# Fetching modulation matrix tiles one product ahead, spreading their products over four blocks, and storing the HGRN masks once

## The chip, the cores and the metric

The kernel runs on one core of one Trainium2 chip. The metric is the device time of one execution in microseconds (us); for several runs the median is given. All other times below are read from one profiled execution.

## The reference

One decoder layer over 2048 positions of width 1024. What matters here is the modulation vector, the in-projection that it feeds, and the three mixers behind it:

```python
c_act = jax.nn.silu(c)
mod = c_act @ ada_w[l] + ada_b[l]
sh1, sc1, g1, sh2, sc2, g2 = [m[:, None, :] for m in jnp.split(mod, N_MOD, axis=-1)]
h = rmsnorm(x, norm_mix_w[l]) * (1.0 + sc1) + sh1
proj = h @ w_in[l]
o_a = hgrn2_mixer(hq, hf, hi, hg, lower_bounds[l], hg_onorm_w[l])
o_b = dsa_mixer(sq, sk, sv, iq, ik, iw)
o_c = conv_module(cu, cv_w[l], cv_b[l], cv_ln_w[l], cv_ln_b[l])
x = x + g1 * (jnp.concatenate([o_a, o_b, o_c], axis=-1) @ w_out[l])
h = rmsnorm(x, norm_mlp_w[l]) * (1.0 + sc2) + sh2
x = x + g2 * (jnp.square(jax.nn.relu(h @ mlp_w1[l])) @ mlp_w2[l])
```

`ada_w` is a 1024 x 6144 matrix in f32. Sections 0 and 1 (`sh1`, `sc1`) are needed before the first in-projection; sections 2 to 5 (`g1`, `sh2`, `sc2`, `g2`) only behind the in-projection. The HGRN mixer works in chunks of 128 positions and masks its products level by level with 0/1 masks (`lmask`), one for each of five levels.

## The kernel before

**Blocks.** The 2048 positions are four blocks of 512. `in_block(b, ...)` runs the in-projection of a block as 26 units: each unit is a matmul against one slice of `w_in` (L357, or L1165 for the wide ones), followed by an evacuation (`ev_hf`, `ev_hq`, `ev_ca` ...). After the fourth block come the out-projection and the MLP, which use sections 2 to 5 of the modulation.

**Work beside the units.** At each bare `yield` of `in_block`, `step()` gives a credit in ns to seven queues of generators (`rates`): `fast` (HGRN, `hgrn_gen`), `conv` (`conv_gen`), `ada` (`ada_gen`), `idx`, `tk`, `at` (indexer, top-k, attention) and `ts`. A generator runs as long as its queue has credit and says at each yield how much that piece costs. So the order of the program is: unit, evacuation, some HGRN, some conv, some modulation, and so on. From this order a planner lays out one instruction order for each engine; it may put an instruction ahead of earlier ones if its inputs and its buffer are there, and it plans with its own durations. On the chip each engine runs its instructions strictly in that order, SyncE (SP) its DMA issues too.

**Modulation, sections 2 to 5.** `ada_gen` walks 4 sections x 4 column slices of 256. Each slice is a sum of 8 products, done by `ada_part`: for k in 0..7 it takes a 128 x 256 tile of `ada_w` (128 KB, tag `adw`, AB = 2 buffers) by a DMA on SP (L186) and multiplies it on VectorE (DVE) by one column of `cact`, at L188 for k = 0 and at L190 (multiply and add into `adacc`, one buffer) for the other seven. Then TensorE (PE) sums over partitions: at L707 into one row in sections 2 and 5, to which L710 adds a slice of `ada_b` (tile `adrow`, which has the tag `adw` too) before a DMA stores it in `g_d`; at L198 into columns in sections 3 and 4, read by L199. Both take a bank of the tag `mm`, which the units of the in-projection use as well. A product asks for 1.2 x 256 = 307.2 ns of credit; the rate is 800 a step. `ada_gen` is queued in block 1 (behind unit 2, event "idx"), and at the event "prep" (block 3, ahead of unit 14) the queue is drained.

**Conv.** `conv_gen` multiplies 31 taps into two accumulators: half of the taps on DVE (L530, 128 x 512, `cacc`), half by ScalarE (ACT) and GpSimd (POOL) (L527, L528).

**HGRN.** `hgrn_gen` works on one head of a block. Per level it multiplies q and k by gates (L604, L605; the factor is read by repeat), PE makes the level's product (L639, L647), and for levels 0 to 4 DVE copies the masked part (L620, L641, `copy_predicated`). `lmask` holds 5 x 256 bytes per partition: the mask of 64 columns, four times over. It is made at the start by `late_consts` with a 128 x 256 work tile `mwork` (tag `r`, one buffer; L445 to L450). The head's result is a tile `r` of the same tag (L694), stored to `mx_d` by a DMA.

## Time and profile before

| what | value |
|---|---|
| time, median of 3 runs | 3066.41 us (3060.03 to 3070.0) |
| time of the profiled execution | 3064.96 us |
| its span, first to last instruction | 3063.2 us |
| mean granted TensorE clock | 0.966 of 2.4 GHz |
| PE busy | 2831.0 us, 92% of the span |
| DVE busy | 1982.8 us, 65% |
| POOL busy | 1792.8 us, 59% |
| ACT busy | 1541.4 us, 50% |
| DMA, share of 16 engines' time in the main queue | 57.5% |

The profiled execution lies 1.45 us below the median, inside the spread of the runs; 1.8 us of it lie outside the span. PE, DVE, ACT, POOL and SP are the five engines; a name such as "DVE k L605" is the instruction of line 605 on VectorE that writes tile `k`. "A <- B" in a list of waits means that A's engine sat idle until B was done. "PEclk" is the share of full clock granted to TensorE.

### The profile page before, as it was taken

To read this page: it belongs to the slowest core of one execution; us is meant where nothing else is said; L and a number is where in the kernel's file an instruction comes from. 1 tells how busy PE (TensorE), PEld (TensorE's weight loads), DVE (VectorE), ACT (ScalarE), POOL (GpSimd) and SP (SyncE) were. 2 spreads that over 40 slices of the span, in tenths; PEclk is the share of its full clock that TensorE was granted. 3 is DMA by queue.
4 is the path that set the end of the run, shared out by engine and by line. 5 is a ranking of instruction groups with operands and counts; after the bars stand their busy time and mean duration, and the time that the engine had idled before them with its cause. 6 is when DMAs were issued, how large, how long until landed. Compare 5 with 4: busy or idle time off the path is not lost.

```text
span 3063.2 us, 50800 instructions
## 1 busy us (share of the span) xinstructions
PE 2831.0 (92%) x18352; PEld 2554.6 (83%) x18352; DVE 1982.8 (65%) x3673; ACT 1541.4 (50%) x2883; POOL 1792.8 (59%) x1530
## 2 busy tenths in 40 slices
PE   6989989898999989999999999998899998989997
PEld 4768868777887889888988899898788887889997
DVE  7796487867536343756667747476979531387787
ACT  3436355445423244555556656555654444456654
POOL 6566152225304265666788666577776756767775
PEclk9989989898999999999999999999999999999999
DMA  7857757565655343444556445344899953465533
GB/s 258 283 183 244 229 182 228 190 202 172 227 185 166 119 156 100 130 126 131 167 154 212 138 135 154 121 157 159 259 302 291 320 184 118 139 196 183 176 125 114
DMA packets 479416, 560.10 MB, mean 183 GB/s; under 512 B 32615, under 2 KB 371884, under 8 KB 479148
## 3 DMA queue, kind: packets, MB, share of 16 engines
q1 hardware_dynamic: 478992, 556.65, 57.5%
q8 instruction: 145, 2.38, 0.3%
q14 instruction: 123, 1.01, 0.1%
q10 hardware_dynamic: 156, 0.07, 0.0%
HBM read 458.30 MB, written 98.31 MB: 182 GB/s over the span
## 4 chain that ended last, share of the span: by engine, by line
PE 47%; DVE 8%; DMA 4%; issue 4%; POOL 3%; ACT 2%; SPq 1%; DVEq 0%; POOLq 0%; ACTq 0%
PE ax L1165 18%; PE mm L357 14%; PE ix L752 1%; PE po L939 1%; PE at L905 1%; PE at L927 1%; DMA tsr<-in_mlp_w_dram 1%; PE mm L1165 1%; PE at L1165 1%; POOL wlo L264 1%; PE ax L1530 1%; PE at L1541 1%; PE ax L1541 1%; SPq L106 1%; PE at L1530 1%
## 5 line engine op out<-in xcount | busy, mean ns | idle before, releaser
L264 POOL TENSOR_TENSOR wlo<-wraw,whi 128x512 fp32r<-128x512 f32 x514 | 719.3, 1420 | 406.8 <-ACT whi L256 269.6
L256 ACT CAST whi<-wraw 128x1024 fp32r<-128x1024 f32 x257 | 269.5, 1049 | 329.0 <-PE ax L1165 137.8
L759 DVE SCALAR_TENSOR_TENSOR s<-r,iw_s,s 128x512 f32<-128x512 f32 (+3 forms) x266 | 261.9, 984 | 209.7 <-ACT r L754 208.5
L1165 PE MATMUL ax<-whi,hh 128*128 128x256 f32 x1600 | 282.5, 290 | 30.4 <-DVE acc L1309 20.7
L357 PE MATMUL mm<-ah,wk 128*128 128x512 f32 x1104 | 299.3, 407 | 9.0 <-ACT k L577 3.5
L1165 PE MATMUL ax<-whi,hl 128*128 128x256 f32 x1600 | 280.5, 288 | 2.4 <-POOL hl L264 2.4
L1165 PE MATMUL ax<-wlo,hh 128*128 128x256 f32 x1600 | 274.0, 287 | 0.0
L937 POOL TENSOR_TENSOR pT<-L,pT 128x512 fp32r<-128x512 f32 (+3 forms) x160 | 197.5, 1237 | 130.7 <-ACT pT L936 111.2
L1165 PEld LDWEIGHTS ax<-whi,hh 128*128 128x128 f32 x1600 | 235.8, 193 | 39.8 <-DVE acc L1309 19.6
L357 PE MATMUL mm<-ah,whi 128*128 128x512 f32 x936 | 255.7, 399 | 10.3 <-DVE slo L470 3.0
L357 PE MATMUL mm<-al,whi 128*128 128x512 f32 x936 | 258.6, 398 | 0.0
L357 PEld LDWEIGHTS mm<-ah,wk 128*128 128x128 f32 x1104 | 208.2, 194 | 55.1 <-ACT k L577 4.5
L357 PE MATMUL mm<-ah,wlo 128*128 128x512 f32 x936 | 253.0, 394 | 0.0
L1165 PEld LDWEIGHTS ax<-whi,hl 128*128 128x128 f32 x1600 | 233.5, 193 | 5.6 <-POOL hl L264 3.2
L1165 PEld LDWEIGHTS ax<-wlo,hh 128*128 128x128 f32 x1600 | 231.2, 193 | 2.6
L754 ACT ACTIVATE r<-ix 128x512 f32<-128x512 f32 (+3 forms) x256 | 141.2, 552 | 181.2 <-PE ix L752 168.3
L528 POOL TENSOR_TENSOR cside<-cside,ctap 128x512 f32<-128x512 f32 x112 | 161.3, 1440 | 115.0 <-ACT ctap L527 92.0
L357 PEld LDWEIGHTS mm<-ah,whi 128*128 128x128 f32 x936 | 174.2, 190 | 47.1 <-DVE slo L470 3.9
L357 PEld LDWEIGHTS mm<-al,whi 128*128 128x128 f32 x936 | 176.2, 191 | 35.3
L357 PEld LDWEIGHTS mm<-ah,wlo 128*128 128x128 f32 x936 | 175.1, 189 | 35.9
L1309 DVE TENSOR_TENSOR acc<-acc,ax 128x512 f32<-128x512 f32 x160 | 109.1, 682 | 96.4 <-PE ax L1165 96.1
L857 DVE TENSOR_SCALAR_CACHE_REDUCE cum<-s,ssm 128x384 bf16<-128x384 f32 (+13 forms) x112 | 165.2, 1475 | 5.0 <-POOL s L763 3.1
(552 smaller groups left out, 6842.6 us busy)
## 6 DMA issues: line engine op xcount, KB each, us to landing
wraw<-in_mlp_w_dram SPq DMA_DIRECT2D x192, 512.0 KB
wk<-wk_d SPq DMA_DIRECT2D x174, 512.0 KB
kc<-sk_d SPq DMA_DIRECT2D x112, 256.0 KB
vc<-v_d SPq DMA_DIRECT2D x112, 256.0 KB
tsr<-in_mlp_w_dram SPq DMA_DIRECT2D x96, 256.0 KB
ts_d<-tsr SPq DMA_DIRECT2D x48, 512.0 KB
wr<-in_mlp_w_dram SPq DMA_DIRECT2D x96, 256.0 KB
wr<-ts_d SPq DMA_DIRECT2D x72, 256.0 KB
```

The lines of the kernel that those rows point to most:

```text
L256: A.copy(hi, src)
L264: e.tensor_tensor(lo[:, i:j], src[:, i:j], hi[:, i:j].bitcast(F32), OP.subtract)
L357: T.matmul(ps, ww[:, k, :], aa[k], start=(n == 0 and k0 == 0), stop=(n == len(order) - 1 and k1 == NK))
L528: G.tensor_tensor(side, side, tap, OP.add)
L754: A.activation(r[:, :w], ps[:, :w], AF.Relu, scale=32.0 ** -0.5)
L759: V.scalar_tensor_tensor(s[:, c0:c0 + w], r[:, :w], iw, s[:, c0:c0 + w], op0=OP.mult, op1=OP.add)
L857: V.tensor_scalar(dump, s, t, -AIM - i * STEP, op0=OP.is_ge, op1=OP.add, accum_out=d)
L937: G.tensor_tensor(pT[:, :nt, 1], lv, pT[:, :nt, 0].bitcast(F32), OP.subtract)
L1165: T.matmul(ps[:, t * 256:(t + 1) * 256], aa[f][:, tok * P:(tok + 1) * P], ww[:, f, :], start=(first and n == 0 and (last or t == 0)), stop ...
L1309: V.tensor_tensor(dst, dst, src, OP.add)
L1530: T.matmul(dst, ww[:, k, :], av[k][p], start=(first and n == 0), stop=(n == 11), skip_group_check=True)
L1541: T.matmul(dst[:, t], av[k][p][:, t * P:(t + 1) * P], ww[:, k, :], start=(first and n == 0), stop=(n in (5, 11)), skip_group_check=True)
```

## The change

1. The tiles of `ada_w` come from a generator of their own, `ada_tiles`, which allocates a tile and issues its DMA one product before that tile is handed out. `adw` gets 3 buffers instead of 2.
2. `adrow` takes the tag `r` (the HGRN result's, one buffer) instead of `adw`.
3. `ada_gen` is queued in block 0 instead of block 1, and its rate is 400 a step instead of 800.
4. `lmask` holds the 64 columns of each mask once and is read by repeat (a step of 0) at L620 and L641; `mwork` shrinks to 128 x 64 with it.

```diff
-WQ, AQ, AB = 0, 0, 2
+WQ, AB = 0, 3
...
-    def ada_part(pool, wtag, wbufs, acc, sec, c0, w):
+    def ada_tiles():
+
+        todo = [(sec, c0, k) for sec in (2, 4, 3, 5) for c0 in range(0, D, AW) for k in range(NK)]
+        ahead = []
+        for sec, c0, k in todo:
+            t = hp.tile([P, AW], F32, tag="adw", bufs=AB, name=nm("adw"))
+            dma(t, ada2[k * P:(k + 1) * P, sec * D + c0:sec * D + c0 + AW])
+            ahead.append(t)
+            if len(ahead) > 1:
+                yield ahead.pop(0)
+        yield ahead.pop(0)
+
+    def ada_part(acc, tiles):
         for k in range(NK):
-            t = pool.tile([P, w], F32, tag=wtag, bufs=wbufs, name=nm("adw"))
-            (nc.gpsimd if AQ else nc.sync).dma_start(t, ada2[k * P:(k + 1) * P, sec * D + c0:sec * D + c0 + w])
+            t = next(tiles)
             if k == 0:
                 V.tensor_scalar(acc, t, cact[:, 0:1], None, op0=OP.mult)
             else:
                 V.scalar_tensor_tensor(acc, t, cact[:, k:k + 1], acc, op0=OP.mult, op1=OP.add)
-            yield 1.2 * w
+            yield 1.2 * AW
...
-    lmask = cst.tile([P, 5, 256], U8, name="lmask")
+    lmask = cst.tile([P, 5, 64], U8, name="lmask")
...
-        mwork = hp.tile([P, 256], F32, tag="r", bufs=1, name="mwork")
+        mwork = hp.tile([P, 64], F32, tag="r", bufs=1, name="mwork")
...
-            G.affine_select(mwork, mwork, pattern=[[0, 4], [-2 * h, ng], [0, h]],
+            G.affine_select(mwork, mwork, pattern=[[-2 * h, ng], [0, h]],
...
-                              lmask[:, 0, :128].rearrange("p (c g) -> p c g", c=2), pv[:, :, P:])
+                              lmask[:, 0:1, :].to_broadcast([P, 2, 64]), pv[:, :, P:])
...
-                                  lmask[:, l, :].rearrange("p (c g e) -> p c g e", c=4, e=hs), psv)
+                                  lmask[:, l:l + 1, :].rearrange("p o (g e) -> p o g e", e=hs)
+                                  .to_broadcast([P, 4, gc, hs]), psv)
...
     def ada_gen():
+        tiles = ada_tiles()
...
-                yield from ada_part(hp, "adw", AB, acc, sec, c0, AW)
+                yield from ada_part(acc, tiles)
...
-                    row = hp.tile([1, AW], F32, tag="adw", bufs=AB, name=nm("adrow"))
+                    row = hp.tile([1, AW], F32, tag="r", bufs=1, name=nm("adrow"))
...
-    rates = {"fast": FAST, "conv": CR, "ada": 800.0, "ts": 1.0, "idx": R1[0], "tk": R1[1], "at": R1[2]}
+    rates = {"fast": FAST, "conv": CR, "ada": 400.0, "ts": 1.0, "idx": R1[0], "tk": R1[1], "at": R1[2]}
...
                 if b == 0:
                     add_topk(k1, (2, 3))
+                    queues["ada"].append(ada_gen())
                 if b == 1:
                     add_topk(k1, range(4, J1))
-                    queues["ada"].append(ada_gen())
```

## Rows read from the trace of the kernel before

**Rows 1.** The page's first part: busy time of each engine and its share.

```profile
PE 2831.0 (92%) x18352; PEld 2554.6 (83%) x18352; DVE 1982.8 (65%) x3673; ACT 1541.4 (50%) x2883; POOL 1792.8 (59%) x1530
```

**Rows 2.** Blocks 0 to 3: stretch, length, PE, PEld, DVE, ACT, POOL busy, PEclk, DMA share, GB/s.

```profile
65.00:307.00 242.00, 217.68 (x1213) 186.50 (x1214) 181.96 (x375) 118.32 (x218) 145.66 (x124) 0.94 0.72 233
307.00:576.00 269.00, 246.16 (x1447) 209.70 (x1447) 191.93 (x471) 131.50 (x297) 87.15 (x99) 0.94 0.65 205
576.00:843.00 267.00, 243.36 (x1445) 207.32 (x1445) 181.79 (x428) 121.78 (x265) 93.72 (x93) 0.95 0.63 203
843.00:1085.00 242.00, 232.13 (x1465) 206.06 (x1464) 117.99 (x219) 69.23 (x155) 71.11 (x63) 0.98 0.48 157
```

**Rows 3.** Waits of DVE from 0 to 1150 us: total, times, longest.

```profile
DVE adacc L190 <- DMA adw<-in_ada_w_dram: 57.9, 38, 6.4
```

**Rows 4.** Waits of PE from 307 to 843 us (blocks 1 and 2): total, times, longest.

```profile
PE ax L647 <- DVE k L605: 11.5, 3, 4.6
```

**Rows 5.** Instructions on tile adw: durations ns min/median/max, first and last start.

```profile
L190 DVE SCALAR_TENSOR_TENSOR adacc<-adw,cact,adacc x112: 469/485/1615, 50.9 to 776.3; 128x256 f32<-128x256 f32 x112
```

**Rows 6.** DVE in order of time, block 1: start, length, [idle before <- ended by].

```profile
385.67 0.48 DVE L190 SCALAR_TENSOR_TENSOR adacc<-adw,cact,adacc 128x256 f32<-128x256 f32 x1 [1.88 <-DMA adw<-in_ada_w_dram]
...
388.14 0.52 DVE L190 SCALAR_TENSOR_TENSOR adacc<-adw,cact,adacc 128x256 f32<-128x256 f32 x1 [1.26 <-DMA adw<-in_ada_w_dram]
```

**Rows 7.** PE in order of time, block 1.

```profile
397.59 3.78 PE L357 MATMUL mm<-ah,wk 128*128 128x512 f32 x8 [3.04 <-ACT k L577]
...
426.06 0.92 PE L647 MATMUL ax<-q,k 128*64 128x64 f32 x8 [4.36 <-DVE k L605]
```

**Rows 8.** DVE in order of time, block 2: first and last of four waits.

```profile
736.97 0.48 DVE L190 SCALAR_TENSOR_TENSOR adacc<-adw,cact,adacc 128x256 f32<-128x256 f32 x1 [2.95 <-DMA adw<-in_ada_w_dram]
...
742.00 0.48 DVE L190 SCALAR_TENSOR_TENSOR adacc<-adw,cact,adacc 128x256 f32<-128x256 f32 x1 [0.88 <-DMA adw<-in_ada_w_dram]
```

**Rows 9.** PE in order of time, block 2.

```profile
752.11 0.80 PE L905 MATMUL at<-kc,qs 128*128 128x256 f32 x2 [5.04 <-DVE mx L907]
```

**Rows 10.** Two stretches of 10 us, columns as in Rows 2.

```profile
390.00:400.00 10.00, 6.70 (x30) 4.96 (x29) 10.00 (x14) 6.27 (x11) 5.32 (x5) 0.78 0.55 183
...
750.00:760.00 10.00, 7.89 (x47) 7.90 (x47) 6.52 (x19) 2.61 (x6) 2.85 (x4) 0.66 0.42 139
```

**Rows 11.** The conv stretch of each block, columns as in Rows 2.

```profile
120.00:190.00 70.00, 58.93 (x261) 47.21 (x262) 69.39 (x120) 27.53 (x49) 44.67 (x33) 0.88 0.61 199
390.00:434.00 44.00, 30.99 (x148) 23.05 (x146) 44.00 (x73) 22.09 (x40) 23.34 (x21) 0.83 0.52 164
660.00:720.00 60.00, 52.47 (x263) 41.33 (x262) 57.43 (x102) 29.30 (x61) 30.98 (x26) 0.89 0.56 183
910.00:955.00 45.00, 39.06 (x194) 30.94 (x193) 44.23 (x58) 15.83 (x26) 21.43 (x15) 0.96 0.41 131
```

**Rows 12.** The same stretches of blocks 1 and 2, tile adacc alone: PE, PEld, DVE busy.

```profile
390.00:434.00 44.00, 1.40 (x4) 0.17 (x4) 7.92 (x9) 0.83 0.52 164
660.00:720.00 60.00, 1.63 (x6) 0.70 (x6) 12.07 (x16) 0.89 0.56 183
```

**Rows 13.** Groups by line, until 307 us and in block 1: busy, mean ns | idle before.

```profile
L190 DVE SCALAR_TENSOR_TENSOR adacc<-adw,cact,adacc 128x256 f32<-128x256 f32 x7 | 5.3, 760 | 0.1
...
L190 DVE SCALAR_TENSOR_TENSOR adacc<-adw,cact,adacc 128x256 f32<-128x256 f32 x56 | 33.2, 593 | 33.4 <-DMA adw<-in_ada_w_dram 33.1
```

**Rows 14.** Tile lmask's largest group, columns as in Rows 5.

```profile
L641 DVE COPY_PREDICATED at<-lmask,ax x64: 418/436/754, 113.8 to 1107.7; 128x256 f32<-128x256 uint8 x64
```

**Rows 15.** DVE in order of time: the start, then two 256-wide operations of block 1.

```profile
29.26 0.29 DVE L450 CAST lmask<-mwork 128x256 uint8<-128x256 f32 x1 [0.54 <-POOL mwork L448]
...
392.46 0.41 DVE L605 TENSOR_TENSOR k<-k,fb 128x256 f32<-128x256 f32 x1
...
407.24 0.41 DVE L655 TENSOR_TENSOR fb<-f 128x256 f32<-128x256 f32 x1
```

**Rows 16.** Waits of SP's DMA queue from 307 to 790 us: total, times, longest.

```profile
SPq L186 <- DVE adacc L190: 46.8, 43, 5.2
```

More of the change, by code (lines that the diff above doesn't have):

```diff
@@ L445, in late_consts @@
             V.memset(mwork, 1.0)
-            G.affine_select(mwork, mwork, pattern=[[0, 4], [-2 * h, ng], [0, h]],
+            G.affine_select(mwork, mwork, pattern=[[-2 * h, ng], [0, h]],
                             compare_op=OP.is_ge, fill=0.0, base=0, channel_multiplier=1)
-            G.affine_select(mwork, mwork, pattern=[[0, 4], [2 * h, ng], [0, h]],
+            G.affine_select(mwork, mwork, pattern=[[2 * h, ng], [0, h]],
                             compare_op=OP.is_gt, fill=0.0, base=h, channel_multiplier=-1)
```

## The prediction

> **What bounds the kernel now.** The page's first part comes first: PE is busy 92% of the span and no other engine is over 65% [rows 1]. So a microsecond on another engine counts only where PE then stands still, or where the granted clock falls behind such a stall. The change touches the start and the four in-projection blocks alone, so next I read the blocks [rows 2]. Blocks 1 and 2, which hold all but the first eight of the 128 products, leave PE idle 22.8 and 23.6 us. Block 0, without those, is no better: 24.3 us. Block 3, without modulation and with little attention beside it, has 9.9 us. DVE's busy time goes with that: 182, 192, 182 and 118 us.
>
> Who waits for whom is the third view. Over the in-projection DVE stands still 57.9 us, in 38 waits, for `adw` tiles [rows 3]; PE itself never waits for them, but for DVE's later work, above all L605 [rows 4]. A DVE wait costs something only if it stands ahead of a PE stall with no slack between. Two places in the order of time show that. In block 1, waits of 1.88 and 1.26 us [rows 6] open a run in which DVE has no more idle time until 434 us, and in that run PE stalls, 3.04 and 4.36 us at the two largest [rows 7]. In block 2, four waits that add up to 4.97 us (first and last of the four in [rows 8], the other two are of 0.54 and 0.60 us) come before a PE stall of 5.04 us that DVE's L907 ends [rows 9]. Behind these stalls the granted clock is 0.78 and 0.66 of 2.4 GHz in the 10 us around them [rows 10]: part of that time is at the level of 1.2 GHz.
>
> **The change part by part.**
>
> *Prefetch.* Before, SP issues tile k+2 only when product k has freed its buffer: its L186 waited 46.8 us for L190 [rows 16], and the product that follows meets a tile still in flight. With a third buffer and one product ahead, three tiles are under way instead of two. At 1.3 products a step of 8 to 9 us (400 / 307.2; 242 us / 29 steps in block 0), a product comes every 6.4 to 7 us, longer than any wait of the 38 (6.4 us at most). I take the waits as gone. What it is worth is the part that stands before a stall: 1.88 + 1.26 in block 1 and 4.97 in block 2, 8.1 us. The clock behind them lost (1 - 0.78) x 10 = 2.2 and (1 - 0.66) x 10 = 3.4 us; the stalls of block 1 don't vanish, so I take half of 5.6. Together -8.1 - 2.8 = **-10.9 us**; bounds 0 (another releaser is as late) and -13.7.
>
> *Spread.* In program order the products go from 0, 68, 60, 0 in the four blocks to 34, 38, 38, 18 (26, 29, 29 and 15 steps). What counts is the conv stretch of each block, where DVE is busy 96 to 100% and PE idles 11.1, 13.0, 7.5 and 5.9 us [rows 11]. There the modulation now takes 0, 7.92, 12.07 and 0 us of DVE [rows 12]. After, at a product every 6.4 us in block 0 and 7.1 us in the others, the stretches hold 11, 6, 8 and 6 of them instead of 0, 9, 16 and 0. A product costs 0.76 us by the mean of the few in block 0 and 0.59 in block 1 [rows 13]; in the stretches themselves 7.92 / 9 = 0.88 and 12.07 / 16 = 0.75. So DVE's load there moves by +11 x 0.76 = +8.4, -3 x 0.88 = -2.6, -8 x 0.75 = -6.0 and +6 x 0.75 = +4.5, in sum +4.3 us. How much reaches PE: in the stretches PE idles 37.5 us of 219 (the four of [rows 11]), far less than DVE is full, so a DVE microsecond is not a PE microsecond. Between 0 (a product fits where DVE idles soon after the stretch) and 1 with the clock on top, I take half and a third of that again for the clock: **+2.9 us**; bounds 0 and +12.
>
> *What a product costs in block 0.* The row: L190 takes 0.469 us at best, 0.485 in the median and 1.615 at most [rows 5], and POOL, which reads SBUF too, is busy 60% of block 0 against 32% of block 1 [rows 2]; the means stand in the same order. The Trainium skill (SBUF — State Buffer, "SBUF: two separate sides") says that a VectorE operation with two SBUF inputs and a GpSimd operation that reads SBUF exclude one another for the whole instruction. That speaks against moving products into the block where GpSimd is busiest. By the rule, with half of a 1.3 us POOL operation to wait out in 60% of cases, an estimate from that page's rule is 0.48 + 0.39 = 0.87 us a product, and the stretch of block 0 would take 9.6 us instead of 8.4; the trace agrees as far as its means go.
>
> *Row tile on tag `r`.* Eight `adrow` tiles now share one buffer with the 16 HGRN results. A row's load waits on SP until the last result is stored, with the weights queued behind it, and the next L694 on DVE waits until the row is stored. No row of before shows that wait. It is nothing if the planner has a row and a result apart; at the worst it is a wait like those of the `adw` tiles, 57.9 / 38 = 1.5 us, for each of eight rows, half of them before a stall: +6 us. I take 0, since results are a head apart (some 65 us) and a row lives a few us.
>
> *Masks.* Ten POOL and ten DVE operations at the start get a quarter as wide. DVE waited 0.54 us for one of them and spent 0.29 on the copy [rows 15], in the chain that leads to the first projections; there are five. I take **-1.5 us**, bounds 0 and -3. Reading by repeat: the 64 L641 take 0.436 us in the median [rows 14]; none of before repeats a mask. The nearest is L605, which reads a factor by repeat and takes 0.41 us, as L655 does with plain inputs of the same width [rows 15]. So 0; if 0.03 us came on each of 96 (L641's 64 and L620's 32), +3 us of DVE, of which half at most counts.
>
> *DMA.* Block 0 gets 26 more tiles of 128 KB, 3.4 MB beside the 56 MB that it moves (233 GB/s x 242 us): the share goes from 0.72 to some 0.76. The cover is the weights' own lead: no weight's DMA stands among PE's waits there. 0; without that cover, 3.4 MB at 233 GB/s are 15 us of transfer.
>
> Sum against the profiled execution: 3064.96 - 10.9 + 2.9 - 1.5 = 3055.5. That execution lies 1.45 us below the median of the runs, which is less than their spread, so I leave it: **3055 us**, 0.37% under the median. Its own range, with all bounds: -16.7 to +22.5, say 3048 to 3080, the upper part only if the price of block 0 goes to its bound.
>
> **The rivals.**
>
> *Block 0 decides (slower).* Its conv stretch has DVE busy 69.4 of 70 us with PE idle 11.1 already [rows 11]; nothing is left there to hide 11 products, and two slice sums fall into it, each holding one of the units' two `mm` banks until DVE adds the row. If each added microsecond reaches PE, with half again for the clock (0.88 there already), block 0 costs 8.4 x 1.5 = 12.6 and block 3, in the same way, 4.5 x 1.5 = 6.8; blocks 1 and 2 give back the waits without the clock, 8.1. Sum +11: **3076 us**. It decides from the point where PE's idle time between 120 and 190 us grows beyond some 20 us. For it: the full DVE. Against: DVE has half of the 10 us after 190 us free, and block 1 with 7.9 us of products in 44 us has only 2 us more PE idle than block 0's stretch.
>
> *The waits change places.* Where DVE doesn't wait for a tile it runs into the next wait of its strict order, for PE or ACT, and the stalls stay: block 0 has as much PE idle without any tile to wait for. Gain 0 there, the spread about 0: **3065 us**.
>
> *The prefetch doesn't do what it says.* The planner may already lay products in bursts as soon as buffers are free, so that three buffers only shorten the waits (57.9 x 2/3 = 39 us left), and one product ahead is no time ahead. A third of the 8.1 us is won: **3062 us**.
>
> *More than counted.* The whole run of stalls in block 1 (13.0 us idle, clock 0.83 over 44 us = 7.5 us) and the one of block 2 (5.0 + 3.4) go: -25, **3040 us**.
>
> **How the numbers follow.** Chances: forecast 0.47, block 0 decides 0.22, waits change places 0.15, prefetch idle 0.08, more than counted 0.08. About 0.3% (9 us) is what a measurement of this kernel can tell from no change. The forecast lies at that edge: I give its chance as 0.28 faster, 0.17 same, 0.02 slower. With 0.08 of the last rival and 0.04 of the two small ones, faster is 0.40; same is 0.17 + 0.19 and 0.02 of the block 0 case, 0.38; slower the rest, 0.22. The range takes in both neighbours, from near the large gain to beyond the slower case: 3042 to 3080.
>
> **What would show it.** Right: the `adw` waits of DVE fall below 15 us; the stall at 752 us is gone and the clock of its 10 us near 1; PE idle in blocks 1 and 2 falls by 4 to 5 us each and in block 0 rises by no more than 5. Wrong: PE idle in block 0 up by 9 us or more; new waits of L694 for the row's store; L641 slower than 0.44 us; or waits of the same size in blocks 1 and 2 with another releaser. A different order that the planner lays out for work the change doesn't touch would make the whole sum wrong.

## The result, and the profile after

The changed kernel takes **3099.27 us** (median of 4 runs, 3093.52 to 3101.09) against 3066.36 us beside it: a ratio of **1.0105 [1.0088, 1.0121]**. It is slower by 1%, 44 us above the forecast and outside the range. Lines move with the change: L190 is now L201, L605 L616, L641 L652, L694 L706, L707 L720, L710 L723, and the DMA on SP L106.

The page's first part of the profile after, beside [rows 1]: with as many instructions PE is busy 9.3 us longer and DVE 15.7; the span is 3097.0, 33.8 us longer.

```profile
PE 2840.3 (92%) x18352; PEld 2556.1 (83%) x18352; DVE 1998.5 (65%) x3673; ACT 1536.8 (50%) x2885; POOL 1778.9 (57%) x1530
```

Where do 33.8 us lie? Busy times by stretch, columns as in Rows 2: the in-projection (up to the fourth store of `x_d`), the MLP of the first block (up to its fourth store of the output), and the rest, first before and then after.

```profile
0.00:1105.90 1105.90, 993.78 (x5872) 856.87 (x5872) 727.74 (x1594) 472.80 (x977) 457.03 (x442) 0.95 0.63 203
1105.90:1655.00 549.10, 528.02 (x3394) 478.24 (x3395) 345.09 (x691) 305.62 (x552) 373.28 (x321) 0.98 0.47 144
1655.00:3063.20 1408.20, 1309.24 (x9087) 1219.52 (x9085) 909.93 (x1390) 763.00 (x1355) 962.50 (x769) 0.97 0.58 183
```

```profile
0.00:1135.30 1135.30, 1004.25 (x5874) 867.37 (x5875) 731.22 (x1594) 473.93 (x981) 446.40 (x442) 0.94 0.61 197
1135.30:1690.50 555.20, 530.90 (x3409) 479.06 (x3409) 350.46 (x697) 308.45 (x554) 370.16 (x321) 0.98 0.47 143
1690.50:3097.00 1406.50, 1305.12 (x9073) 1209.67 (x9071) 916.77 (x1383) 754.46 (x1352) 962.35 (x769) 0.97 0.59 182
```

The in-projection is 29.4 us longer, the first MLP block, whose code is untouched, is 6.1 us longer, and the rest is 1.7 us shorter. Now the four blocks of after, to be read against [rows 2] (a block runs here from ACT's first write of tile `kst` to the next one, the last to the fourth store of `x_d`; the same bounds in before give 242.3, 269.7, 265.6 and 262.8 us, behind a start of 65.5, now 60.5):

```profile
60.50:343.10 282.60, 235.68 (x1261) 198.24 (x1260) 208.23 (x426) 124.05 (x232) 147.48 (x131) 0.89 0.67 219
343.10:599.50 256.40, 239.15 (x1409) 205.97 (x1407) 175.57 (x425) 134.29 (x295) 85.28 (x95) 0.95 0.61 196
599.50:866.60 267.10, 240.09 (x1428) 208.73 (x1428) 174.08 (x402) 115.36 (x259) 91.20 (x92) 0.94 0.59 195
866.60:1135.30 268.70, 253.59 (x1634) 224.94 (x1634) 129.76 (x251) 75.78 (x165) 86.14 (x79) 0.97 0.48 157
```

**Block 0 is 40.3 us longer.** PE idles 282.6 - 235.7 = 46.9 us in it instead of 24.2, and the granted clock is 0.89 instead of 0.94 over a longer time: (1 - 0.89) x 282.6 = 31 us lost instead of 15. A part is work that changed sides of the mark: block 0 holds 1261 matmuls, and 1217 before by the same bounds. Block 1 gives 13.3 us back, block 2 has 1.5 more, block 3 has 5.9 more.

The waits of DVE and of PE from 0 to 1150 us (total, times, longest), beside [rows 3, 4]:

```profile
DVE adacc L201 <- DMA adw<-in_ada_w_dram: 40.8, 24, 5.5
```

```profile
PE ax L650 <- DVE k L616: 28.0, 8, 8.9
```

The waits for `adw` fell from 57.9 to 40.8 us only. PE's waits for DVE's gates, the second fence, grew to 28.0 us (behind L605 before they were 21.0 over the same stretch).

### The profile page after: what moved, and what is told of

It is laid out like the page before. It is cut to its first block, busy times and chain, and to the rows that moved or that the text cites. A ratio compares the mean times of both kernels' runs of the same rounds, so it can differ in the third digit from the quotient of the medians.

```text
span 3097.0 us, 50847 instructions
## 1 busy us (share of the span) xinstructions
PE 2840.3 (92%) x18352; PEld 2556.1 (83%) x18352; DVE 1998.5 (65%) x3673; ACT 1536.8 (50%) x2885; POOL 1778.9 (57%) x1530
## 4 chain that ended last, share of the span: by engine, by line
PE 56%; DVE 19%; DMA 8%; issue 6%; POOL 6%; ACT 3%; SPq 1%; DVEq 0%; POOLq 0%; ACTq 0%
PE mm L368 20%; PE ax L1178 17%; PE mm L1178 3%; DVE cacc L541 3%; POOL wlo L275 2%; DMA adw<-in_ada_w_dram 2%; PE po L952 2%; PE ix L765 1%; DVE s L772 1%; PE at L940 1%; DVE cum L870 1%; PE ax L650 1%; PE at L918 1%; DMA wraw<-in_mlp_w_dram 1%; SPq L106 1%
## 5 line engine op out<-in xcount | busy, mean ns | idle before, releaser
L275 POOL TENSOR_TENSOR wlo<-wraw,whi 128x512 fp32r<-128x512 f32 x514 | 721.9, 1425 | 447.6 <-ACT whi L267 316.8
L368 PE MATMUL mm<-ah,wk 128*128 128x512 f32 x1104 | 298.8, 406 | 8.2 <-ACT k L588 2.2
L368 PE MATMUL mm<-ah,whi 128*128 128x512 f32 x936 | 264.5, 406 | 8.7 <-DVE q L597 5.3
L1178 PEld LDWEIGHTS ax<-whi,hh 128*128 128x128 f32 x1600 | 236.0, 193 | 35.8 <-DVE acc L1322 13.7
L368 PE MATMUL mm<-al,whi 128*128 128x512 f32 x936 | 255.3, 397 | 0.0
L368 PE MATMUL mm<-ah,wlo 128*128 128x512 f32 x936 | 252.8, 394 | 0.0
L368 PEld LDWEIGHTS mm<-ah,wk 128*128 128x128 f32 x1104 | 209.0, 194 | 52.6 <-ACT k L588 2.6
L368 PEld LDWEIGHTS mm<-ah,whi 128*128 128x128 f32 x936 | 176.4, 194 | 46.5 <-DVE q L597 5.7
L368 PEld LDWEIGHTS mm<-al,whi 128*128 128x128 f32 x936 | 176.5, 191 | 36.2
L368 PEld LDWEIGHTS mm<-ah,wlo 128*128 128x128 f32 x936 | 175.2, 189 | 36.1
## 6 DMA issues: line engine op xcount, KB each, us to landing
wraw<-in_mlp_w_dram SPq DMA_DIRECT2D x192, 512.0 KB
wk<-wk_d SPq DMA_DIRECT2D x174, 512.0 KB
ts_d<-tsr SPq DMA_DIRECT2D x48, 512.0 KB
```

The lines of the kernel that those rows point to most:

```text
L275: e.tensor_tensor(lo[:, i:j], src[:, i:j], hi[:, i:j].bitcast(F32), OP.subtract)
L368: T.matmul(ps, ww[:, k, :], aa[k], start=(n == 0 and k0 == 0), stop=(n == len(order) - 1 and k1 == NK))
L1178: T.matmul(ps[:, t * 256:(t + 1) * 256], aa[f][:, tok * P:(tok + 1) * P], ww[:, f, :], start=(first and n == 0 and (last or t == 0)), stop ...
```

## The experiments

The first theory was the one of the rival "block 0 decides": DVE's time for products in the conv stretch of block 0 reaches PE. Its rivals were the order that the planner lays out anew, and later a bank of PSUM (the memory that PE's sums go to) that is held. "Held" means: it contains a sum that is finished but not yet read. All eighteen kernels in one table. "Block 0" and "0+1" are lengths in us of the profiled execution; "held" is the longest time, among the first four slice sums, from PE's sum (L707 / L720) to the row's add on DVE (L710 / L723) where the sum stands in a bank of tag `mm`. Each ratio is to the kernel before on the same chip.

| run | what | median us | ratio [95%] | block 0 | 0+1 | held |
|---|---|---|---|---|---|---|
| before | | 3066.36 | 1 | 242.3 | 512.0 | 9.0 |
| c1_repeat | before, masks read by repeat | 3068.38 | 0.9996 [0.9982, 1.0011] | 245.3 | 514.4 | 9.0 |
| n1_rate790 | before, rate 790 | 3085.3 | 1.0059 [1.0036, 1.0082] | 245.3 | 516.5 | 9.0 |
| c2_narrow | before, narrow `mwork` | 3093.1 | 1.0072 [1.0055, 1.0090] | 235.7 | 537.1 | 5.1 |
| e3_masks | before, whole mask part | 3085.36 | 1.0054 [1.0035, 1.0074] | 233.5 | 531.0 | 4.4 |
| e1_nospread | after, not spread | 3078.19 | 1.0037 [1.0022, 1.0051] | 232.9 | 530.2 | 36.3 |
| x4_prefetch | e1 with wide `mwork` | 3090.98 | 1.0071 [1.0051, 1.0091] | 253.2 | 549.5 | 29.1 |
| e4_blocks123 | after, products from block 1 | 3063.81 | 0.9990 [0.9972, 1.0007] | 235.3 | 525.5 | 42.6 |
| x2_late0 | after, products from the end of block 0 | 3070.58 | 1.0015 [1.0002, 1.0028] | 232.4 | 527.6 | 31.7 |
| h4_blocks123_rowadw | e4, row on `adw` | 3083.82 | 1.0064 [1.0043, 1.0086] | 242.0 | 514.4 | 4.0 |
| h5_blocks123_sumbank | e4, sums on `at` | 3060.01 | 0.9973 [0.9962, 0.9985] | 234.1 | 508.1 | none |
| h6_late0_sumbank | x2, sums on `at` | 3061.4 | 0.9974 [0.9963, 0.9985] | 234.3 | 514.7 | none |
| e2_spread | before, spread | 3089.85 | 1.0072 [1.0044, 1.0100] | 257.5 | 519.7 | 8.6 |
| h1_rowadw | after, row on `adw` | 3083.91 | 1.0052 [1.0032, 1.0072] | 263.1 | 521.2 | 8.5 |
| h2_sumbank | after, sums on `at` | 3085.18 | 1.0067 [1.0050, 1.0083] | 251.2 | 510.7 | none |
| h3_thin_sumbank | h2, thin products | 3081.74 | 1.0052 [1.0036, 1.0069] | 251.1 | 503.7 | none |
| after | | 3099.27 | 1.0105 [1.0088, 1.0121] | 282.6 | 539.0 | 35.6 |
| x1_thin | after, thin products | 3087.45 | 1.0058 [1.0041, 1.0075] | 276.6 | 536.1 | 34.1 |
| x3_widestart | after, wide `mwork` | 3102.58 | 1.0113 [1.0086, 1.0140] | 280.6 | 545.9 | 41.0 |
| n2_rate410 | after, rate 410 | 3108.85 | 1.0127 [1.0104, 1.0149] | 272.5 | 545.3 | 39.9 |

### One part at a time

**e1_nospread**: the changed kernel with rate and block of before.

```diff
-"ada": 400.0
+"ada": 800.0
...
-                if b == 0:
+                if b == 1:
                     queues["ada"].append(ada_gen())
```

> The changed kernel with the spread alone undone: rate 800, queued in block 1; prefetch, third buffer, row on tag r and small masks stay. Theory 'block 0' (the products moved into block 0, where VectorE is full, cost the 33 us): 3048 to 3066 us, block 0 back at about 242 us, and what the prefetch brings alone is seen. Theory 'prefetch or masks' (the loss comes from the buffers and tags): 3085 to 3100 us. Theory 'any new order costs' (the planner's order changes everywhere): somewhere between, with block 0 still longer than 250 us.

**e2_spread**: before with the spread alone.

```diff
-"ada": 800.0
+"ada": 400.0
...
-                if b == 1:
+                if b == 0:
                     queues["ada"].append(ada_gen())
```

> The kernel before with the spread alone: rate 400, queued in block 0; two buffers, no prefetch, masks four times over. Theory 'block 0': 3090 to 3105 us, block 0 some 280 us, as in the changed kernel. Theory 'prefetch or masks': 3060 to 3070 us. Theory 'any new order costs': between, 3070 to 3090 us.

**e3_masks**: before with the whole mask part and nothing else.

```diff
-    lmask = cst.tile([P, 5, 256], U8, name="lmask")
+    lmask = cst.tile([P, 5, 64], U8, name="lmask")
...
-        mwork = hp.tile([P, 256], F32, tag="r", bufs=1, name="mwork")
+        mwork = hp.tile([P, 64], F32, tag="r", bufs=1, name="mwork")
...
-                                  lmask[:, l, :].rearrange("p (c g e) -> p c g e", c=4, e=hs), psv)
+                                  lmask[:, l:l + 1, :].rearrange("p o (g e) -> p o g e", e=hs)
+                                  .to_broadcast([P, 4, gc, hs]), psv)
```

> The kernel before with the masks alone stored once and read by repeat (and the narrower work tile at the start). Theory 'block 0' and my sum: 3062 to 3066 us, a start some 1 to 5 us shorter, nothing else. Theory 'prefetch or masks': up to 3095 us, with L641's masked copies slower than 0.44 us. Theory 'any new order costs': 3070 us or more although no instruction is slower.

**e4_blocks123**: the changed kernel, its products spread over blocks 1 to 3.

```diff
-"ada": 400.0
+"ada": 562.0
...
-                if b == 0:
+                if b == 1:
                     queues["ada"].append(ada_gen())
```

> The changed kernel with its products spread over blocks 1 to 3 alone: rate 562, queued in block 1. Theory 'block 0': 3045 to 3065 us, since block 0 keeps its 242 us and blocks 1 and 2 have fewer products than before. Theory 'prefetch or masks': 3085 us or more. Theory 'any new order costs': 3070 to 3090 us, with block 0 longer than before although it holds no more products.

Measured were ratios of 1.0037, 1.0072, 1.0054 and 0.9990. The spread alone (e2) costs most, but everything without it (e1) and the masks alone (e3) cost 0.4 and 0.5% too, and these don't add up: the masks, ten smaller operations at the start and a different reading pattern, stand with 19 us. e1 came as none of its theories had it: block 0 is back at 232.9 us, and the kernel is still 11 us slower. e2 and e3 came as the theory "any new order costs" had it, though block 0 of e2 grew by 15 us too. Keeping products out of block 0 (e4) takes the whole loss away.

### Is it the work, or the order that is laid out?

**c1_repeat**: before with the repeat reading alone, from a full `lmask`. **c2_narrow**: before with the 64-wide `mwork` alone, copied out four times. **n1_rate790**: before with one number changed, as a control: 2.57 products a step instead of 2.60. **n2_rate410**: the same to the changed kernel. The edits of c1, c2, n1 and n2:

```diff
-                                  lmask[:, l, :].rearrange("p (c g e) -> p c g e", c=4, e=hs), psv)
+                                  lmask[:, l:l + 1, :64].rearrange("p o (g e) -> p o g e", e=hs)
+                                  .to_broadcast([P, 4, gc, hs]), psv)
```

```diff
-        mwork = hp.tile([P, 256], F32, tag="r", bufs=1, name="mwork")
+        mwork = hp.tile([P, 64], F32, tag="r", bufs=1, name="mwork")
...
-            V.tensor_copy(lmask[:, l, :], mwork)
+            V.tensor_copy(lmask[:, l, :].rearrange("p (c n) -> p c n", c=4), mwork[:, None, :].to_broadcast([P, 4, 64]))
```

```diff
-"ada": 800.0
+"ada": 790.0
```

```diff
-"ada": 400.0
+"ada": 410.0
```

> The kernel before, in which L620 and L641 read the first 64 columns of each mask by repeat; the masks are still made and stored four times over. It tells what of the 19 us of the masks alone is the reading. Theory 'a repeated read is slower': 3080 us or more and L641 above 0.46 us. Theory 'the planner's order': L641 stays at 0.43 to 0.44 us, and the time moves, if at all, by another releaser's waits; I expect 3060 to 3080 us.

> The kernel before, with the masks made in a 64 wide work tile and then copied out four times; stored and read as before. Theory 'a repeated read is slower': 3062 to 3067 us, since the reading is as before. Theory 'the planner's order, set off by a shorter start': as slow as the masks alone, 3075 to 3090 us, with block 1 some 20 us longer than in the kernel before and no L641 slower.

> The kernel before with the rate of the modulation at 790 instead of 800: 2.57 products a step instead of 2.60, nothing else. A control: no step of my sum moves by more than 1 us. If the time stays within 9 us of 3066, a difference of 19 or 33 us is not the planner's scatter; if it moves by 15 us or more, a change of a few products in the order is worth as much as the masks are.

> The changed kernel with the rate at 410 instead of 400, a control like 790 for 800: 1.33 products a step instead of 1.30. No step of any theory moves by more than 1 us. If the changed kernel's 33 us are in what it does, 3090 to 3105 us; if they are the planner's scatter, anything from 3070 to 3110 us.

Measured were 0.9996, 1.0072, 1.0059 and 1.0127. c1, c2 and n1 came as the order theories had it, c2 3 us above its range; n2, at 3108.85, lies 4 us above the range of the first of its theories and inside the wide one of the second, scatter. Reading by repeat is free; the groups on tile `lmask` in c1 and in after (columns as in Rows 5; 436 ns in [rows 14]):

```profile
L641 DVE COPY_PREDICATED at<-lmask,ax x64: 415/435/745, 114.6 to 1106.1; 128x256 f32<-128x256 uint8 x64
```

```profile
L652 DVE COPY_PREDICATED at<-lmask,ax x64: 410/439/747, 91.7 to 1137.8; 128x256 f32<-128x256 uint8 x64
```

In c1 PE, DVE, ACT and POOL run the instructions of before in the same order, one by one, and the time is the same. In n1 and c2 no step that matters is changed, but the planner lays out another order, and the time is 18 and 22 us longer. Windows of n1 over the same three stages show where: the in-projection is 5.4 us longer than before and the first MLP block, which holds no modulation work at all, 7.8.

```profile
0.00:1111.30 1111.30, 1000.63 (x5872) 862.68 (x5872) 738.65 (x1594) 470.99 (x975) 462.13 (x442) 0.94 0.63 202
1111.30:1668.20 556.90, 534.08 (x3408) 482.35 (x3409) 354.38 (x698) 308.60 (x556) 371.56 (x321) 0.98 0.48 143
1668.20:3079.60 1411.40, 1306.96 (x9073) 1212.14 (x9071) 912.99 (x1384) 754.58 (x1352) 961.11 (x769) 0.98 0.59 182
```

In c2 PE in order of time meets stalls for a transfer; PE's waits of this kind add up to 11.0 us in the in-projection of c2 and to 1.3 in that of before:

```profile
512.33 0.76 PE L752 MATMUL at<-ki,qi 96*128 96x512 f32 x1 [5.40 <-DMA ki<-ki_d]
531.83 0.47 PE L752 MATMUL at<-ki,qi 96*128 96x256 f32 x2 [3.21 <-DMA ki<-ki_d]
```

So before's order is a good one among its neighbours, and a difference of 0.6% between two kernels with different orders doesn't show by itself that a part of the change caused it. What can be trusted is a place where the same thing happens in each kernel of a group.

### Products in block 0

**x1_thin**: the first 34 products of the changed kernel one column wide, except the first of each slice, so 29 of them; the other columns of these products are left out. **x2_late0**: products queued behind block 0's conv stretch, rate 500. **x3_widestart**: the changed kernel with the 256-wide `mwork`. **x4_prefetch**: e1 with the 256-wide `mwork`, that is, before with prefetch, third buffer, row on `r` and masks stored once. The edits of x1 (`done` counts the products), then x2, then the first line of the one that x3 and x4 share (the masks are again made 256 wide, and 64 columns of them are stored):

```diff
-            V.scalar_tensor_tensor(acc, t, cact[:, k:k + 1], acc, op0=OP.mult, op1=OP.add)
+            m = 1 if done[0] <= 34 else AW
+            V.scalar_tensor_tensor(acc[:, :m], t[:, :m], cact[:, k:k + 1], acc[:, :m], op0=OP.mult, op1=OP.add)
```

```diff
-"ada": 400.0
+"ada": 500.0
...
                     add_topk(k1, (2, 3))
-                    queues["ada"].append(ada_gen())
...
                 if b == 0:
+                    queues["ada"].append(ada_gen())
                     queues["at"] += [attn_gen(k1, 0), attn_gen(k1, 1)]
```

```diff
-        mwork = hp.tile([P, 64], F32, tag="r", bufs=1, name="mwork")
+        mwork = hp.tile([P, 256], F32, tag="r", bufs=1, name="mwork")
```

> The changed kernel in which the first 34 products (those of block 0) multiply and add 1 column instead of 256, except the first product of each slice; the DMAs, the sums on TensorE and the rest stay. Columns 1 to 255 of those slices thus lack seven of their eight products. Theory 'block 0' (VectorE's time there is the price): block 0 falls from 283 us to 250 us or less and the time to 3070 us or less. Theory 'the order alone': the time stays within 10 us of 3099, as 30 instructions of 0.6 us are a small part of what was lost.

> The changed kernel with the modulation queued at the event qkv of block 0 (behind unit 22, when block 0's conv is over) instead of behind unit 2, rate 500: block 0 holds some 8 products ahead of its conv stretch and some 6 behind it, none inside. Theory 'block 0's full VectorE': most of what the spread costs goes, 3060 to 3075 us, block 0 below 255 us. Theory 'order alone': 3085 to 3100 us, as with any other order.

> The changed kernel, its masks stored once and read by repeat, but made in the wide work tile as before, so that the start's instructions are those of before. The narrow start alone cost 22 us and the repeated reading nothing. Theory 'the narrow start re-lays the order, and the costs add': 3075 to 3085 us. Theory 'any order but the one of before costs about the same': 3090 to 3105 us, as the changed kernel.

> The kernel before with the prefetch alone: a tile one product ahead, three buffers, the row on tag r; masks stored once (which was free) but made in the wide work tile; products in blocks 1 and 2 at the rate 800. My sum: 3053 to 3060 us, VectorE's waits for tiles below 20 us. 'The waits change places': 3062 to 3070 us with those waits at 30 us or less. 'A new order costs': 3075 us or more.

Measured were 1.0058, 1.0015, 1.0113 and 1.0071. x2 came as the theory of block 0 had it, x3 and x4 as the order theories had it. The products in block 0's conv stretch are needed for the loss in block 0 (x2, e4), whatever the start looks like (x3). x1 came as neither of its theories had it: block 0 takes 276.6 us instead of 282.6, with 46.3 us of PE idle instead of 46.9. But it can't say what the products' time on DVE costs, since the edit hardly took that time away. L201 takes 25.6 us in block 0 of after. In x1 it is L205, and this is its row there; the second fence has two of its thin products and the POOL operation ahead of them in order of time:

```profile
L205 DVE SCALAR_TENSOR_TENSOR adacc<-adw,cact,adacc 128x1 f32<-128x1 f32 (+1 forms) x30 | 17.3, 578 | 11.6 <-DMA adw<-in_ada_w_dram 11.2 <-DVE adacc L205 0.3
```

```profile
175.85 1.34 POOL L543 TENSOR_TENSOR cside<-cside,ctap 128x512 f32<-128x512 f32 x1
...
176.50 0.71 DVE L205 SCALAR_TENSOR_TENSOR adacc<-adw,cact,adacc 128x1 f32<-128x1 f32 x1
...
178.70 0.20 DVE L205 SCALAR_TENSOR_TENSOR adacc<-adw,cact,adacc 128x1 f32<-128x1 f32 x1
```

A thin product takes some 0.2 us where it doesn't meet POOL. Of the 29, 12 last 0.7 to 1.3 us, and each of these ends within 0.02 us of a POOL operation that ran when it began. So x1 saved 8.3 us of DVE in block 0, and not the 16 that 24 thin products there would save at 0.2 us each in place of 0.85 (an estimate from these rows). Whether DVE's load reaches PE stays open here; the trace of after shows another cost of the same products.

### The held bank

It stands in the order of time of after, engines PE, DVE and SP, around the second slice sum:

```profile
164.98 0.59 PE L720 MATMUL mm<-adacc,ones 128*1 128x256 f32 x2
...
183.71 0.75 DVE L706 SCALAR_TENSOR_TENSOR r<-ax,cols,gate 128x512 f32<-128x512 f32 x1
...
185.49 0.52 SPq L106 DMA_DIRECT2D mx_d<-r  x1
...
191.01 0.24 SPq L106 DMA_DIRECT2D adrow<-in_ada_b_dram  x1
...
195.84 0.40 DVE L723 TENSOR_TENSOR adrow<-mm,adrow 1x256 f32<-1x256 f32 x1
```

PE sums the slice at 165 us into a bank of `mm`. The row's slice of `ada_b` must be loaded into the one buffer of tag `r`, which belongs to a head's result first: it is made at 183.7, stored from 185.5, and only then the row is loaded (191.0) and added (195.8). For 30.9 us the sum holds one of the two `mm` banks that the projection works with. The next two sums of block 0 hold theirs 32.3 and 35.6 us, and two later rows 19.7 us in block 2 and 28.0 in block 3; before, with the row on `adw`, the longest of all eight was 9.0. The list of waits on tile `adrow` from 100 to 350 us shows none of it:

```profile
  DMA adrow<-in_ada_b_dram: 0.3, 1
  PE mm L720: 0.2, 1
```

The instruction that ends the hold never waits long, as it is laid out late on DVE. What the hold does shows in the order of the units. DVE reads a unit's sum at L481, and only then PE begins the next unit (L368):

```profile
173.86 0.68 DVE L481 TENSOR_TENSOR slo<-mm,shi 128x512 fp32r<-128x512 f32 x1
...
174.59 3.50 PE L368 MATMUL mm<-ah,whi 128*128 128x512 f32 x8
...
182.38 0.69 DVE L481 TENSOR_TENSOR slo<-mm,shi 128x512 fp32r<-128x512 f32 x1
...
183.17 2.14 PE L368 MATMUL mm<-ah,whi 128*128 128x512 f32 x8
```

Between 165.1 and 174.6 us PE runs no matmul of a unit, and its waits there (6.5 us behind L684) are those of HGRN's products, the work that was left to it. Through all three holds PE begins no new sum in `mm` before the last read of the one ahead of it. PE in the three holds (windows, columns as in Rows 2):

```profile
165.20:195.80 30.60, 21.13 (x86) 16.83 (x85) 30.56 (x61) 10.66 (x24) 19.76 (x16) 0.81 0.72 232
233.60:265.70 32.10, 26.61 (x146) 22.55 (x144) 21.51 (x52) 9.93 (x25) 16.74 (x15) 0.89 0.78 250
291.80:327.10 35.30, 24.94 (x145) 20.62 (x141) 24.00 (x56) 21.70 (x49) 14.49 (x18) 0.85 0.50 163
```

They are 98 us of the block's 282.6, and hold 25.3 of its 46.9 us of idle time and 5.8 + 3.5 + 5.3 = 14.6 of its 31 us of lost clock. Four kernels test it. **h1_rowadw** puts the row back on `adw`; **h2_sumbank** leaves it on `r` and takes the sum's bank from `at`; **h3_thin_sumbank** does so with thin products (a tile is 256 columns wide, not 400 as its text says); **h4_blocks123_rowadw** is e4 with the row on `adw`.

```diff
-                    row = hp.tile([1, AW], F32, tag="r", bufs=1, name=nm("adrow"))
+                    row = hp.tile([1, AW], F32, tag="adw", bufs=AB, name=nm("adrow"))
```

```diff
-XP = '0111000000000111'
+XP = '0112000000000211'
```

> The changed kernel with one line put back: the row of a finished slice takes a buffer of tag adw (three buffers) again, and not the one buffer of tag r. Theory 'held bank': in the changed kernel the bank of a slice's sum in tag mm is held from PE's sum (L720) to VectorE's row add (L723) for 30.9, 32.3 and 35.6 us in block 0, since the row waits for HGRN's result in r; with one of two mm banks gone the projection runs single-banked. Then here the holds fall under 10 us, block 0 falls from 282.6 us to about 258 (what spreading alone, whose row is on adw, shows: 257.5), PE's idle and slow-clock loss in it from 77.6 to about 55, and the time to about 3075. Theory 'products in block 0': VectorE's products and the order laid out around them are the loss, the hold is a by-stander: holds fall, block 0 stays over 272 us, the time 3090 to 3105.

> The changed kernel with the PSUM tiles of the slices' sums (and of the rows' turn) taken from tag at, which the in-projection uses little, in place of mm; the row stays on r. Theory 'held bank': the holds stay some 30 us long but hold no bank of the projection: block 0 falls to 255 to 262 us and the time to 3070 to 3080. Theory 'products in block 0': no fall, block 0 over 272 us, 3090 to 3105. If this one falls and the row on adw does not, it was the row's buffer on adw that costs something of its own.

> The changed kernel with its first 34 products computed on one column in place of 400 (the rest of their columns is left out, so what these products should add is missing) and the slices' sums on tag at: both suspected costs of block 0 taken away. With thin products alone block 0 stood at 276.6 us, 3087.45. If VectorE's time and the held bank are the whole of block 0's loss, its length falls to 240 to 250 us and the time to 3055 to 3070. If the order that is laid out around the products is the loss, block 0 stays over 265 us and the time over 3080.

> The changed kernel with the products queued at block 1 at rate 562 (3063.81 so far) and the row on tag adw. There block 1 takes 290.2 us against 269.7 before, with four holds of 26.5, 7.2, 29.6 and 42.6 us. Theory 'held bank': the holds go, block 1 falls by 10 to 20 us and the time to 3045 to 3055, faster than before. Theory 'order': block 1 and the time move by less than 10 us in either direction.

Block 0 of h1, h2, h3 and x1, one fence each (columns as in Rows 2):

```profile
61.50:324.50 263.00, 227.44 (x1241) 191.80 (x1240) 198.48 (x409) 122.66 (x229) 146.22 (x129) 0.90 0.73 234
```

```profile
63.10:314.30 251.20, 219.69 (x1212) 184.73 (x1211) 195.68 (x406) 118.67 (x215) 151.09 (x128) 0.92 0.75 241
```

```profile
63.80:314.90 251.10, 222.17 (x1244) 187.12 (x1243) 194.99 (x409) 124.04 (x230) 148.61 (x129) 0.95 0.76 241
```

```profile
61.70:338.30 276.60, 230.32 (x1273) 194.14 (x1272) 201.43 (x439) 127.41 (x238) 145.03 (x134) 0.92 0.70 222
```

Block 0 falls from 282.6 to 263.1 and to 251.2 us, and PE's idle time in it from 46.9 to 35.6 and 31.5; the rest of the fall is a better clock and, by the counts, 20 and 49 matmuls that moved out of the block. In h2 the sums wait even longer for their rows, in order of time on PE and DVE:

```profile
209.25 1.01 PE L720 MATMUL at<-adacc,ones 128*1 128x256 f32 x2 [5.84 <-DVE adacc L201]
...
276.68 0.41 DVE L723 TENSOR_TENSOR adrow<-at,adrow 1x256 f32<-1x256 f32 x1
```

That is 67 us, and block 0 is 31 us shorter all the same; PE waits 0.9 us for a bank so held, once. In its second hold (180 to 220 us) PE begins a unit while the one ahead of it is still to be read by DVE:

```profile
183.14 1.05 PE L368 MATMUL mm<-ah,whi 128*128 128x512 f32 x2
...
189.85 0.68 DVE L484 SCALAR_TENSOR_TENSOR slo<-mm,shi 128x512 fp32r<-128x512 f32 x1
```

So in block 0 it was the bank and not the wait. h3 is nearly h2 again, as its thin products still take 23.1 us of DVE in block 0, against 26.6 in h2; its 0.1 us says little about DVE's time. It missed the forecast of its first theory (240 to 250 us, 3055 to 3070) and came at 3081.74. The whole time fell by less than the block, from 1.0105 to 1.0052 and 1.0067, so that in h1 and h2 block 0 moved as the bank theory had it or more, and the time came out between the two theories. In the profiled executions block 3 of h1 is 280.6 us instead of 268.7, and behind the in-projection each has an order of its own. (The profiled execution of h1, 3097.9 us, is the highest of its four.)

In h4 the hold goes as expected, from 42.6 to 4.0 us, and block 1 falls from 290.2 to 272.4 us, but block 2 rises from 242.9 to 273.9 and the time comes out at 3083.82 instead of 3045 to 3055. Blocks 1 and 2, e4 and then h4:

```profile
298.80:589.00 290.20, 256.96 (x1532) 217.34 (x1530) 219.45 (x549) 151.92 (x339) 99.38 (x114) 0.97 0.58 187
589.00:831.90 242.90, 229.30 (x1392) 198.46 (x1392) 159.80 (x331) 104.37 (x232) 86.06 (x82) 0.97 0.66 214
```

```profile
303.30:575.70 272.40, 246.35 (x1425) 210.37 (x1423) 187.36 (x438) 136.62 (x305) 92.90 (x101) 0.93 0.61 189
575.70:849.60 273.90, 246.42 (x1450) 213.75 (x1451) 176.41 (x424) 116.34 (x263) 91.03 (x91) 0.94 0.61 197
```

Part of that is work that changes sides of the mark: PE ran 1532 and 1392 matmuls in the two, then 1425 and 1450. A block's length alone isn't a gain where the mark between two blocks moves.

### Without either cost

**h5_blocks123_sumbank** and **h6_late0_sumbank** are e4 and x2 with the sums on `at`.

> The changed kernel with the products queued at block 1 at rate 562 and the slices' sums on tag at. Without the latter it took 3063.81 with block 1 at 290.2 us. Theory 'held bank' alone: block 1 falls by 15 to 20 us and the time to 3045 to 3055, faster than before. Theory that the fall is given back by the order that is laid out anew behind it, as in h4 (block 1 from 290.2 to 272.4, block 2 from 242.9 to 273.9): block 1 falls and the time comes out within 3060 to 3085 again.

> The changed kernel with the products queued behind block 0's conv stretch at rate 500 and the slices' sums on tag at. Without the latter it took 3070.58 with block 1 at 295.2 us and four holds of 29.3, 31.7, 3.3 and 31.4 us in it. Theory 'held bank' alone: block 1 falls to 270 to 280 us and the time to 3048 to 3058. Theory that the order gives it back: block 1 falls, a later block grows by as much, and the time stays within 3060 to 3085.

Measured were **0.9973 [0.9962, 0.9985]** and **0.9974 [0.9963, 0.9985]**, the only two kernels of the study whose interval lies below 1: faster than before by a quarter of a per cent and, by the ratios, than the changed kernel by 1.3%. The forecast of 3045 to 3058 that the bank theory made for them was too low: block 1 fell by 16.2 and 14.8 us, and block 2 rose by 21.4 and 22.8, as the second theory had it. To the fourth store of `x_d` h5 and h6 take 1102.5 and 1102.0 us, e4 and x2 1103.4 and 1100.9: by then nothing is left of what the holds in their block 1 cost. Nor is it the bank alone that differs, as in the new order the sums of block 1 come later and wait 2.1 us at most for their rows. The gain over before is smaller than what the order alone has moved in n1 or c2, so the two kernels are better ones, but their 8 us aren't shown to be the prefetch's.

**What follows from all of them.** Read by block 0, the kernels fall into three groups. Without products in its conv stretch it takes 232.4 to 245.3 us (ten kernels and before itself; x4, with 253.2, lies apart and would fall into the second group). With products, but no long hold in `mm`, 251.1 to 263.1 (four; in e2 a bank held for 8.6 us makes PE wait 6.7 us at 177 us). With both, 272.5 to 282.6 (four). In blocks 0 and 1 together, a hold of some 30 us in either stands with 525 to 550 us (eight kernels), none with 504 to 522, except for e3 and c2 (531 and 537). In that sum the products in block 0 cost nothing: with them and without a hold it is 504 to 521, without either 508 to 517, again but for e3 and c2.

By the time the groups are wider. Their mean ratios are 1.0031 without products there (x4 with them, c1 left out as it has before's order; in four of these ten a bank is held in block 1), 1.0061 with products and 1.0101 with both. Up to the fourth store of `x_d`, where all kernels have done the same work, the four with products and no hold take 1114.8 to 1131.1 us and the four with both 1125.5 to 1152.0: on the mean 14.5 us apart, but overlapping, and n2, a meaningless edit, lies 16.7 from after. A hold doesn't always cost, either: block 2 of e1 has two, of 35.8 and 30.0 us, and takes 265.7 us, as before's does with 265.6. And h4, which took the holds out of e4, is the slower of the two.

So it is shown that in block 0 of after PE ran the units on one bank for 98 us and that freeing it shortened the block. That the held bank is some 0.4% of the 1.05% rests on the means; how the rest divides between the products in block 0 and the loss of a favourable order isn't shown.

## Why the prediction was wrong

**The row tile on tag `r`, taken as 0 with a bound of +6, is the step that failed.** Its reasons were true each by itself, a row does live a few us and results are a head apart, and for just that reason a row that stands behind a result waits for a good part of a head, 31 to 36 us in block 0. The prediction looked for the cost in waits of SP and DVE (1.5 us each) and not in what was kept occupied meanwhile. One part of it named the bank: two sums fall into the conv stretch, "each holding one of the units' two `mm` banks until DVE adds the row". It gave the hold no price of its own. With the hold taken away block 0 is 19.5 us (h1) and 31.4 us (h2) shorter, in part by work that moved out of it. The time is 0.5 and 0.4% shorter by the ratios, 16 and 12 us, which is clear of the runs' noise but not of what a new order alone has moved (18 us in n1).

**The bounds** add up to 3087.5 us (22.5 above the profiled execution), and the range ended at 3080; the measured time lies above both.

**Spread, +2.9, bounds 0 to +12.** The count and the time of the products were about right: in 120 to 195 us 13 products took 9.06 us of DVE, against 8.4 us for 11. What that time costs PE isn't shown, as thin products took only 8.3 us of DVE away in x1 (block 0 is 6.0 us shorter) and 3.5 in h3 (0.1 us). With products and no long hold block 0 is on the mean 18 us longer than without, but blocks 0 and 1 together are not longer. The groups of products in block 0 of after and in its other three blocks (busy, mean ns | idle before):

```profile
L201 DVE SCALAR_TENSOR_TENSOR adacc<-adw,cact,adacc 128x256 f32<-128x256 f32 x30 | 25.6, 854 | 8.9 <-DMA adw<-in_ada_w_dram 8.7
...
L201 DVE SCALAR_TENSOR_TENSOR adacc<-adw,cact,adacc 128x256 f32<-128x256 f32 x77 | 46.5, 604 | 32.6 <-DMA adw<-in_ada_w_dram 32.1
```

A product of L201 took 854 ns in block 0, where 760 was taken from seven, and 604 later, where POOL has less to do. The Trainium skill's rule (SBUF — State Buffer, "SBUF: two separate sides") had given an estimate of 870, and the trace agrees with it. So do the thin products above that ended with a POOL operation. What this made of the time isn't shown.

**Prefetch, -10.9.** The waits for `adw` were to fall below 15 us and stood at 40.8 (32.3 in e1, 29.8 in h5). The step of this term that failed is "a product comes every 6.4 to 7 us". The planner lays products in bunches, in after as in before. DVE in order of time:

```profile
176.39 0.47 DVE L201 SCALAR_TENSOR_TENSOR adacc<-adw,cact,adacc 128x256 f32<-128x256 f32 x1
...
177.95 1.51 DVE L201 SCALAR_TENSOR_TENSOR adacc<-adw,cact,adacc 128x256 f32<-128x256 f32 x1
...
180.11 0.47 DVE L201 SCALAR_TENSOR_TENSOR adacc<-adw,cact,adacc 128x256 f32<-128x256 f32 x1
```

From one product to the next it is 1.85 us in the median from 60 us on (2.4 before), and one buffer more did not cover such bunches. This is what the rival "the prefetch doesn't do what it says" had said, with 39 us of waits left. The stall at 752 us [rows 9] went, but block 2 got others, the largest behind top-k and conv operations of DVE with no modulation in them:

```profile
698.87 1.97 PE L650 MATMUL ax<-q,k 128*128 128x64 f32 x8 [8.88 <-DVE k L616]
```

PE idle in blocks 1 and 2 together is 17.3 + 27.0 = 44.3 us instead of 46.5. That block 1 alone fell by 5.6 us, near the 4 to 5 forecast, is no proof, as the marks move and block 2 rose by 3.4. What the prefetch is worth with nothing else wasn't run, and stays open.

**Masks, -1.5.** The start, up to block 0, was 5.0 us shorter in after and 5.1 in c2. But it varies by itself: 60.2 to 63.8 us in the fourteen kernels with the narrow tile, 63.5 to 65.5 in the six with the wide one, on the mean 2.3 us apart, which is inside the bounds of 0 and -3. Whether it reached the end can't be told: x3, without it, took 1.0113 against 1.0105. Repeat reading at 0 was right. **DMA, 0:** right; the one transfer that PE waited for in block 0 of after, 2.5 us for `qs`, has nothing to do with the modulation.

**The rival "block 0 decides"** had the side and the place right. Its mark of some 20 us was not quite met, as PE idles 70.0 - 52.3 = 17.7 us between 120 and 190 us. Its price of +11 was a third of what came; it too counted DVE's microseconds.

**A term that wasn't in the sum at all** is the order of work that the change doesn't touch. The prediction closed with the sentence that a different order would make the sum wrong, and gave it no width; this is the second step that failed. Ten kernels with a new order and no products in block 0's conv stretch lie between 0.9973 and 1.0072: this kernel's neighbours are spread over 1%, and before is near the better end. The range of 38 us would have had to carry some 20 us upwards for that alone.

## What to carry to other kernels

Where a tile changes its tag, ask not how long it lives but what stands before it in the new buffer's turn, and what is held while it waits: a bank of PSUM, held by a sum whose row can't be loaded yet, can cost where the bank is scarce (block 0 here, not block 2 of e1). Such a hold need not show in a list of waits; measure the time from a bank's writer to its last reader. When an experiment is to take an operation's time away, check in its trace that the time went: the thin products kept most of theirs. And where a planner lays out the order anew, run a control with a meaningless edit first: its spread is a width that a forecast should have.

## What the runs showed that was not expected

Of block 0's 40 us only 22.7 are idle time of PE; the rest is busy time, from 44 more matmuls and a lower clock. By the granted clock 31 us were lost beside 46.9 idle in after, 15 beside 24.2 before. Both grew in about the same proportion, but that is no rule: over all twenty kernels the loss in block 0 is 0.3 to 0.8 of its idle time. And a rate of 790 instead of 800, for a queue whose products are over at 776 us in before [rows 5], moved the time by 18 us; in the profiled execution 11 of 16 us lie behind the in-projection.
